# Attention plus gMLP layer on one core: an early pool for the first unit's values, output weights loaded two steps ahead, and four row blocks of the attention output projected among the last units

## The chip, the cores and the metric

The kernel runs on one core of one Trainium2 chip. The metric is the device time of one execution in microseconds (us), the median of three runs. TensorE is written PE, its weight loads PEld, VectorE DVE, ScalarE ACT, GpSimd POOL, and SyncE SP; SPq is SP's instruction queue, from which all the transfers spoken of here are issued.

## The reference, cut to what matters

For 2048 tokens of width 1024, in float32:

```python
y = rms_norm(x, norm_in_g)
q_lat, kv_lat, k_rope, gate_mla, u, v, gate_gmlp = split(y @ w_in)
o_mla  = attention(q_lat, kv_lat, k_rope)          # 8 heads, causal in chunks of 64
o_gmlp = gelu(u) * (w_spatial @ layer_norm(gelu(v)) + b_spatial)
o_mla  = rms_norm(o_mla,  out_norm_mla_g)  * silu(gate_mla)
o_gmlp = rms_norm(o_gmlp, out_norm_gmlp_g) * silu(gate_gmlp)
h = x + concat([o_mla, o_gmlp]) @ w_out
out = rms_norm(h, final_norm_g)
```

## The kernel before, in words

Every product is made of three matmuls on a value split in a high and a low part (`h`, `l`): high by high, high by low, low by high.

**First half** (`with ExitStack() as bs`). Two halves `hf` of 1024 tokens go through the input projections and the low-rank up-projections. Queries, keys and values (high and low) go to DRAM (`qh_d`, `ql_d`, `kh_d`, `kl_d`, `vh_d`, `vl_d`), the gates to `gt_d`. `stage_ug` is the last stage of each half: 8 column chunks by 2 token tiles, each with 48 matmuls (`u` and `g`), 8 small ones (`sp`), and a tail on DVE, ACT and POOL that ends in `zacc`, whose column sums (`zss2`, `zss3`, L87) close the half. The weights of a chunk, `ug0` to `ug7`, lie in `wpool`, three buffers deep. The pool `lp` holds the high and low parts on their way to DRAM. In the second half, ahead of `stage_ug`, the pools on the right side of the memory are closed (`early.close()`) and `kpool`, `qpool` and `mpool` are opened in their room.

**Second half** (`with ExitStack() as at`). Attention goes by 32 units (head `h`, query tile `j` of 512); unit 0 is head 0, tile 3, and the last head goes through its tiles as 3, 2, 1, 0 (units 28 to 31). A unit has `4j + 4` key blocks `kb`: three `ss` matmuls (L793 to L795), exponentials and a split into `ph` and `pl` (ACT, and DVE or POOL by turns), three `po` matmuls (L833 to L835). `ss` has two PSUM buffers. A unit ends in a chain of column sums, reciprocal, `spread` and multiply (`o`, L851), and `o` goes to `ot_d` (L852). `load_unit` loads `ql` (L757), `kl` (L764), `vh` and `vl` (L768) into `vpool`, two units ahead. `row_maxima` makes the row maxima that the exponentials need, some units ahead (`px` on PE, L171; reductions on DVE, L176 and L178).

**What fills PE between key blocks.** After each key block `side()` takes steps of a generator, `filler`: `gmlp_out`, which first makes the gMLP half of the output weights (`out_weights(8)`: load `wos` L865, `woh` on ACT L866, `wol` on DVE L867), then projects the 16 blocks of 128 token rows in 16 steps of three matmuls each (`pg`, L879 to L881) and stores `h1_d`. `tc.issue_after(last.ins)` keeps a step's PE instructions behind that key block's last `ss`. The steps are shared out so that they end with unit 28.

**The end.** After the last unit come `out_weights(0)` and the attention half: `mla_rows(b)` loads `zm` from `ot_d` (L950) and `gm` from `gt_d` (L951), squares, multiplies and splits them (`zmh`, `zml`), and `project` makes block `b` (`pm`, L879 to L881), in the order of the last head's tiles, so the first four blocks are unit 28's rows. Then come the final norm and the store.

**The order of work.** Each queue's order is fixed when the kernel is built: a list scheduler takes, on a simulated timeline, what is ready, earlier lines first; on the chip each queue goes through its list in that order. So a load or a filler step written late can stand early in its queue, and an instruction whose data is late holds up all that stands behind it in its queue.

Of the kernel before, what the change touches and what calls it, by code (L numbers as in the profile page):

```python
# [38 lines left out]
def layer_kernel(ctx: ExitStack, tc: tile.TileContext, a: dict, out: bass.AP):  # L39
# [92 lines left out]
    def load_kh(h, j):  # L132
# [2 lines left out]
        nc.gpsimd.memset(kh[96:100, :].bitcast(F32), 1.0)  # L135
        khs[h, j] = kh

    def max_loads(u):
        h, j = units[u]
        load_qh(h, j)  # L140
        for c in range(j + 1):
            if (h, c) not in khs:
                load_kh(h, c)
# [51 lines left out]
    with ExitStack() as bs:  # L195
# [5 lines left out]
        wpool = pool("wpool", 3)  # L201
        spool = pool("spool", 2)
        tpool = pool("tpool", 2)
        lp = pool("lp", 2)
        up = pool("up", 2)
        early = ExitStack()
        xpool = early.enter_context(tc.tile_pool(name="xpool", bufs=2, side="right"))
        rpool = early.enter_context(tc.tile_pool(name="rpool", bufs=2, side="right"))
        ps_t = early.enter_context(tc.tile_pool(name="ps_t", bufs=3, space=PSUM, side="right"))
        ps_m = pool("ps_m", 5, space=PSUM)  # L210

# [454 lines left out]
        for hf in range(2):  # L666
# [21 lines left out]
            if hf == 1:  # L688
                early.close()
                right_pool("kpool", 7)  # L690
                right_pool("qpool", 6)
                mpool = right_pool("mpool", 3)
                right_pool("ps_x", 2, space=PSUM)
                pools["neg"] = mpool.tile([P, 64], F32, name="neg", bufs=1)
                nc.gpsimd.memset(pools["neg"], NEG)
                pools["mx"] = [mpool.tile([P, 4, 5], F32, name=f"mx{i}", bufs=1) for i in range(3)]
                for m in pools["mx"]:
                    nc.gpsimd.memset(m, NEG)
                pools["mz"] = [mpool.tile([P, P], F32, name=f"mz{i}", bufs=1) for i in range(3)]
                for m in pools["mz"]:  # L700
                    nc.gpsimd.memset(m, 0.0)
            if hf == 0:

                s = spool.tile([P, 1024], F32, tag="stage", name="wsp")
                sv = s.rearrange("p (g t) -> p g t", g=8)
                nc.sync.dma_start(out=sv, in_=a["w_spatial"].rearrange("g s t -> s g t"))
                smask = up.tile([P, P], F32, tag="z", name="smask", bufs=1)
                nc.sync.dma_start(out=smask, in_=a["smask"])
                nc.vector.tensor_mul(sv, sv, smask.unsqueeze(1).broadcast_to([P, 8, P]))
                lnb = spool.tile([P, 1024], F32, tag="stage", name="lnb")  # L710
                nc.sync.dma_start(out=lnb, in_=a["gmlp_ln_b"].partition_broadcast(P))
                diag = rpool.tile([P, 1536], F32, tag="ll", name="diag")
                for c in range(8):
                    nc.vector.tensor_scalar(diag[:, c * P : (c + 1) * P], ident, bsp[:, c : c + 1], None, op0=ALU.mult)
                for g in range(2):
                    pt = ps_t.tile([P, 4, P], F32, tag="pt", name=f"wspt{g}")
                    for i in range(4):
                        nc.tensor.transpose(pt[:, i, :], sv[:, 4 * g + i, :], ident)
                    nc.scalar.copy(wst[:, 4 * g : 4 * g + 4, :], pt)
                for g in range(2):  # L720
                    pt = ps_t.tile([P, 4, P], F32, tag="pt", name=f"rest{g}")
                    for i in range(4):
                        c = 4 * g + i
                        cs = slice(c * P, (c + 1) * P)
                        nc.tensor.matmul(pt[:, i, :], lnb[:, cs], wst[:, c, :], start=True, stop=False)
                        nc.tensor.matmul(pt[:, i, :], ones, diag[:, cs], start=False, stop=True)
                    nc.scalar.copy(rest[:, 4 * g : 4 * g + 4, :], pt)
# [7 lines left out]
    with ExitStack() as at:  # L735
# [2 lines left out]
            return at.enter_context(tc.tile_pool(name=name, bufs=bufs, reuse_waits="tile", **kw))  # L738

        wo = pool("wo", 1)  # L740
        vpool = pool("vpool", 5)
        ppool = pool("ppool", 5)
        wk = pool("wk", 2)
        ep = pool("ep", 1)
# [7 lines left out]

        def load_unit(h, j):

            tok = slice(j * 512, (j + 1) * 512)
            ql = vpool.tile([P, 512], F32R, tag="ql", name=f"ql{h}_{j}", bufs=3)
            nc.sync.dma_start(out=ql[0:QH, :].bitcast(F32), in_=ql_d[h, :, tok])  # L757
            qls[h, j] = ql
            for c in range(j + 1):
                if (h, c) in kls:  # L760
                    continue
                tok = slice(c * 512, (c + 1) * 512)
                kl = vpool.tile([P, 512], F32R, tag="kl", name=f"kl{h}_{c}")
                nc.sync.dma_start(out=kl[0:QH, :].bitcast(F32), in_=kl_d[h, :, tok])  # L764
                kls[h, c] = kl
                vts[h, c] = [vpool.tile([P, 4, P], F32R, tag=tag, name=f"{tag}{h}_{c}") for tag in ("vh", "vl")]
                for dst, src in zip(vts[h, c], (vh_d, vl_d)):
                    nc.sync.dma_start(  # L768
                        out=dst.bitcast(F32),
                        in_=src[tok, h * P : (h + 1) * P].rearrange("(b p) f -> p b f", p=P),  # L770
                    )

        def on_vector(u, nk):

# [82 lines left out]
        nc.vector.tensor_scalar(gout, gout, 0.5, None, op0=ALU.mult)  # L857
        rg = wo.tile([P, NB], F32, name="rg")

        def out_weights(e0):  # L860
            for e in range(e0, e0 + 8):
                s = ep.tile([P, D], F32, tag="ws", name=f"wos{e}", bufs=2)
                wh = wo.tile([P, D], F32R, tag="wh", name=f"woh{e}", bufs=8)
                wl = wo.tile([P, D], F32R, tag="wl", name=f"wol{e}", bufs=8)
                nc.sync.dma_start(out=s, in_=a["w_out"][e * P : (e + 1) * P, :])  # L865
                nc.scalar.activation(wh, s, AF.Copy, scale=gout[:, e : e + 1])  # L866
                nc.vector.scalar_tensor_tensor(  # L867
                    wl, s, gout[:, e : e + 1], wh.bitcast(F32), op0=ALU.mult, op1=ALU.subtract
                )
                yield wh, wl  # L870

        def project(pools, ws, zh, zl, r, xt, nm):
# [19 lines left out]

        def gmlp_out():
            ws = []
            for w in out_weights(8):
                ws.append(w)
                yield
            rsqrt_small(rg, ssz, D, NB)
            for b in range(NB):
# [12 lines left out]
                nc.sync.dma_start(out=h1_d[rows, :], in_=xt)  # L912

        filler = gmlp_out()
        steps = 8 + NB * 16
        weight = [[1 + 6 / (4 * j + 4)] * (4 * j + 4) for _, j in units[: H * NT - 4]]
        weight = [w for ws in weight for w in ws]
        weight += [1.4] * EXTRA
# [7 lines left out]
                next(filler, None)  # L926
                done[1] += 1

        for u in range(2):
            load_unit(*units[u])  # L930
        for u, (h, j) in enumerate(units):
            unit(u, h, j, side)
        for _ in filler:
            pass

        gfin = ep.tile([P, D], F32, tag="zg", name="gfin")
        nc.sync.dma_start(out=gfin, in_=a["final_norm_g"].partition_broadcast(P))
        ws = list(out_weights(0))
        rm = wo.tile([P, NB], F32, name="rm")

        def mla_rows(b):

            rows = slice(b * P, (b + 1) * P)
            zh, zl = [], []
# [1 line left out]
            for g in range(2):  # L946
# [4 lines left out]
                nc.sync.dma_start(out=gm, in_=gt_d[rs, rows].rearrange("(e p) t -> p e t", p=P))  # L951
                nc.scalar.activation(sq[:, 4 * g : 4 * g + 4, :], zm, AF.Square)
                nc.gpsimd.tensor_tensor(zm, zm, gm, op=ALU.mult)
                zh.append(vpool.tile([P, 4, P], F32R, tag="vh", name=f"zmh{b}_{g}"))
                zl.append(vpool.tile([P, 4, P], F32R, tag="vl", name=f"zml{b}_{g}"))
                nc.scalar.copy(zh[g], zm)
                sub_hi(zl[g], zm, zh[g])
            s1 = wk.tile([P, P], F32, tag="s1", name=f"s1_{b}")
# [7 lines left out]
            return zh, zl, xt  # L966

        blocks = [4 * j + k for j in order[H - 1] for k in range(4)]
        ready = mla_rows(blocks[0])
        for n, b in enumerate(blocks):  # L970
            rows = slice(b * P, (b + 1) * P)
            zh, zl, xt = ready
            if n + 1 < NB:
                ready = mla_rows(blocks[n + 1])
            ss = wk.tile([P, 3], F32, tag="fs", name=f"fs{b}")
            junk = ep.tile([P, D], F32, tag="ws", name=f"fj{b}", bufs=2)
            steps = project([px_tile, pe_tile], ws, zh, zl, rm[:, b : b + 1], xt, f"pm{b}")
            for c in range(2):
                cs = slice(512 * c, 512 * c + 512)
                for _ in range(8):  # L980
                    next(steps)
                nc.scalar.activation(junk[:, cs], xt[:, cs], AF.Square, accum_out=ss[:, c : c + 1])
                nc.gpsimd.tensor_scalar(
                    ss[:, 2:3], ss[:, c : c + 1], 1.0 / D, ss[:, 2:3] if c else EPS, op0=ALU.mult, op1=ALU.add
                )
            nc.gpsimd.tensor_tensor(ss[:, 2:3], ss[:, 2:3], mhalf[:, 0:1], op=ALU.pow)
            w = D if n + 1 < NB else 512
            for c in range(0, D, w):
                cs = slice(c, c + w)
                nc.vector.scalar_tensor_tensor(  # L990
                    xt[:, cs], xt[:, cs], ss[:, 2:3], gfin[:, cs], op0=ALU.mult, op1=ALU.mult
                )
                nc.sync.dma_start(out=out[rows, cs], in_=xt[:, cs])


# [68 lines left out]
```

## Time and profile before

| | us |
|---|---|
| median of 3 runs | 1945.61 |
| lowest and highest run | 1943.3 and 1949.13 |
| the profiled execution, its own time | 1944.81 |
| its span, first to last instruction | 1943.0 |
| PE busy in the span | 1888.4 |

The span is 1.8 us shorter than the execution's time. The granted TensorE clock was 0.991 of full speed over the span. A busy PE counts matmuls at either clock, so time lost to a lower clock is busy time too, and is found from the distance between matmuls.

### The profile page before, as it was taken

Reading aid. Unit: us, or ns where it says so; the run is one execution under the profiler, and the core shown is the slowest. Engines: PE = TensorE matmul, PEld = TensorE weight load, DVE = VectorE, ACT = ScalarE, POOL = GpSimd, SP = SyncE. Lnnn points to the kernel's source line nnn. Section 1 sums busy time; section 2 is a strip of 40 time slices with the busy share of each in tenths; the row PEclk is TensorE's granted clock in tenths of the full one; section 3 lists DMA queues with packets and bytes.
Section 4 is the critical chain, followed back from the end, with each engine's and each line's share of the span. In section 5 each row is a group of like instructions: output and inputs, shape, how many; then the busy total and the mean of one; then the engine's idle time right before and its main releaser. Section 6 shows DMA issues by size and latency. Waiting matters only on the chain.

```text
span 1943.0 us, 24726 instructions
## 1 busy us (share of the span) xinstructions
PE 1888.4 (97%) x8558; PEld 1527.0 (79%) x8558; DVE 1166.1 (60%) x2033; ACT 778.0 (40%) x1416; POOL 605.3 (31%) x661
## 2 busy tenths in 40 slices
PE   8999999999999999899998999999999999999998
PEld 6888767888878887688886788888888787767886
DVE  7235454555642454546666877677777777875553
ACT  6232224222422222332213655555555555573332
POOL 5000100122420010001223545554645454564432
PEclk9999999999999999999998999999999999999999
DMA  6226378533322353983216452434425242325652
GB/s 203 93 79 178 95 178 280 148 95 95 103 84 90 86 155 108 233 264 88 85 39 174 130 166 85 125 105 129 124 77 166 71 136 80 95 91 176 196 186 103
DMA packets 238885, 252.44 MB, mean 130 GB/s; under 512 B 18461, under 2 KB 167965, under 8 KB 238761
## 3 DMA queue, kind: packets, MB, share of 16 engines
q1 hardware_dynamic: 238616, 250.86, 43.1%
q8 instruction: 68, 1.11, 0.2%
q14 instruction: 57, 0.46, 0.1%
q10 hardware_dynamic: 144, 0.00, 0.0%
HBM read 158.53 MB, written 92.27 MB: 129 GB/s over the span
## 4 chain that ended last, share of the span: by engine, by line
PE 81%; DVE 6%; DMA 5%; SPq 3%; issue 2%; ACT 2%; POOL 1%; DVEq 0%; POOLq 0%; ACTq 0%
PE px L171 3%; PE po L835 3%; PE ss L793 3%; PE ss L794 3%; PE pm L880 3%; PE pm L881 3%; PE ss L795 3%; PE pm L879 3%; PE po L833 3%; PE pg L879 3%; PE po L834 3%; PE g L112 3%; PE u L111 3%; PE u L110 3%; PE u L112 3%; PE g L110 3%
## 5 line engine op out<-in xcount | busy, mean ns | idle before, releaser
L178 DVE TENSOR_REDUCE mx<-px 128x1 f32<-128x512 f32 (+2 forms) x320 | 178.5, 579 | 19.8 <-PE px L171 17.4
L831 POOL TENSOR_TENSOR accg<-accg,p 128x512 f32<-128x512 f32 (+1 forms) x104 | 119.1, 1145 | 191.2 <-ACT p L825 141.5
L827 POOL TENSOR_TENSOR pl<-p,ph 128x512 fp32r<-128x512 f32 (+1 forms) x128 | 153.4, 1199 | 40.6 <-ACT ph L826 30.2
L77 DVE TENSOR_TENSOR pl<-ss,ph 128x512 fp32r<-128x512 f32 (+2 forms) x160 | 92.8, 580 | 109.7 <-ACT ss L809 103.9
L604 POOL TENSOR_TENSOR z<-gu,ggt 128x512 f32<-128x512 f32 x32 | 41.5, 1295 | 367.4 <-DVE gu L602 200.3
L808 ACT ACTIVATE ph<-ss 128x512 fp32r<-128x512 f32 (+2 forms) x160 | 81.9, 512 | 128.9 <-PE ss L795 119.6
L835 PE MATMUL po<-pl,vh 128*128 128x512 f32 (+1 forms) x320 | 122.6, 383 | 2.4 <-POOL pl L827 1.5
L793 PE MATMUL ss<-qh,kh 100*128 100x512 f32 (+1 forms) x320 | 121.5, 380 | 3.3 <-ACT p L825 3.1
L833 PE MATMUL po<-ph,vh 128*128 128x512 f32 (+1 forms) x320 | 120.5, 376 | 3.7 <-ACT ph L808 3.5
L794 PE MATMUL ss<-ql,kh 96*128 96x512 f32 (+1 forms) x320 | 119.2, 372 | 0.0
L795 PE MATMUL ss<-qh,kl 96*128 96x512 f32 (+1 forms) x320 | 118.0, 369 | 0.0
L834 PE MATMUL po<-ph,vl 128*128 128x512 f32 (+1 forms) x320 | 117.5, 367 | 0.0
L171 PE MATMUL px<-kh,qh 96*128 96x512 f32 (+2 forms) x320 | 110.1, 386 | 6.8 <-DVE mx L178 5.2
L110 PE MATMUL gm<-yh,wh_gm 128*128 128x512 f32 x256 | 101.0, 395 | 4.8 <-DVE kf L402 3.8
L880 PE MATMUL pm<-wol,zmh 128*128 128x512 f32 x256 | 102.2, 399 | 0.0
L881 PE MATMUL pm<-woh,zml 128*128 128x512 f32 x256 | 101.0, 396 | 0.9 <-DVE zml L77 0.9
L879 PE MATMUL pg<-woh,zgh 128*128 128x512 f32 x256 | 101.6, 397 | 0.0
L879 PE MATMUL pm<-woh,zmh 128*128 128x512 f32 x256 | 101.5, 396 | 0.0
L110 PE MATMUL u<-yh,wh_ug 128*128 128x512 f32 x256 | 101.4, 396 | 0.0
L881 PE MATMUL pg<-woh,zgl 128*128 128x512 f32 x256 | 100.8, 394 | 0.0
L880 PE MATMUL pg<-wol,zgh 128*128 128x512 f32 x256 | 100.8, 394 | 0.0
L112 PE MATMUL gm<-yh,wl_gm 128*128 128x512 f32 x256 | 100.5, 392 | 0.0
(713 smaller groups left out, 5021.5 us busy)
## 6 DMA issues: line engine op xcount, KB each, us to landing
ws_ug<-in_w_in SPq DMA_DIRECT2D x32, 512.0 KB, 5.2
xt<-in_x_t SPq DMA_DIRECT2D x16, 512.0 KB, 4.7
gv_d<-gv SPq DMA_DIRECT2D x32, 256.0 KB, 2.0
ws_gm<-in_w_in SPq DMA_DIRECT2D x16, 512.0 KB, 4.2
gt_d<-gth SPq DMA_DIRECT2D x32, 256.0 KB, 2.8
lgv<-gv_d SPq DMA_DIRECT2D x32, 256.0 KB, 2.9
z_d<-z SPq DMA_DIRECT2D x32, 256.0 KB, 2.6
vh<-vh_d SPq DMA_DIRECT2D x32, 256.0 KB, 4.0
```

The lines of the kernel that those rows point to most:

```text
L110: nc.tensor.matmul(ps, wh(d), xh(d), start=(d == 0), stop=False)
L112: nc.tensor.matmul(ps, wl(d), xh(d), start=False, stop=(d == n - 1))
L178: nc.vector.reduce_max(mx[:, b, c + 1 : c + 2], px[:, :w], axis=AX.X)
L793: nc.tensor.matmul(ss[:, l0:], kh[0:100, ks], qh[0:100, l0:], start=True, stop=False)
L794: nc.tensor.matmul(ss[:, l0:], kh[0:QH, ks], ql[0:QH, l0:], start=False, stop=False)
L795: last = nc.tensor.matmul(ss[:, l0:], kl[0:QH, ks], qh[0:QH, l0:], start=False, stop=True)
L833: nc.tensor.matmul(po[:, v0:], vh[:, vs, :], ph[:, v0:], start=(kb == 0), stop=False)
L834: nc.tensor.matmul(po[:, v0:], vl[:, vs, :], ph[:, v0:], start=False, stop=False)
L835: nc.tensor.matmul(po[:, v0:], vh[:, vs, :], pl[:, v0:], start=False, stop=(kb == nk - 1))
L879: nc.tensor.matmul(ps, h, ws[d][0][:, cs], start=(d == 0), stop=False)
L880: nc.tensor.matmul(ps, h, ws[d][1][:, cs], start=False, stop=False)
L881: nc.tensor.matmul(ps, lo, ws[d][0][:, cs], start=False, stop=(d == 7))
```

## The change

It does three things, and moves pools for them.

1. A pool `vfirst` (one buffer of each tag) is opened on the right side after `early.close()`, and ahead of the last `stage_ug` it gets unit 0's `ql` and chunk 0 of head 0's `kl`, `vh` and `vl`. `vpool` goes from 5 buffers to 4 (3 to 2 for `ql`), and each fifth chunk (third `ql`) goes to `vfirst`. `lp` moves to the right side, among the pools that `early.close()` frees, so all pools of the second half lie 8 KB lower in each partition, over other tiles of the first half than before.
2. `out_weights` issues the load of tile `e + 2` after the conversion of tile `e`, instead of each load ahead of its own conversion. For the gMLP half six empty filler steps stand between the first two loads and the first conversion (14 steps instead of 8).
3. `mla_out` is the loop of the end as a generator. Its beginning (`gfin`, `out_weights(0)`, `mla_rows` of the first block) stands ahead of unit 29, and units 29, 30 and 31 take 3, 2 and 3 of its steps after each key block: 12 x 3 + 8 x 2 + 4 x 3 = 64 steps, four blocks of 16. The split rows of the blocks up to number 4, and of every second block behind, lie in `ep` (`zh`, `zl`, room for one block), the others in `vpool`.

The diff, cut to its core:

```diff
+    FIRST = 1
+    def load_ql(h, j):
+        if (h, j) in qls:
+            return
+        pool, bufs = (pools["vfirst"], 1) if len(qls) % 3 == 0 else (pools["vpool"], 2)
+        ql = pool.tile([P, 512], F32R, tag="ql", name=f"ql{h}_{j}", bufs=bufs)
+        nc.sync.dma_start(out=ql[0:QH, :].bitcast(F32), in_=ql_d[h, :, j * 512 : (j + 1) * 512])
+        qls[h, j] = ql
+
+    def load_chunk(h, c):
+        if (h, c) in kls:
+            return
+        pool = pools["vfirst" if len(kls) % 5 < FIRST else "vpool"]
...
-        lp = pool("lp", 2)
...
+        lp = early.enter_context(tc.tile_pool(name="lp", bufs=2, side="right"))
...
                 early.close()
                 right_pool("kpool", 7)
                 right_pool("qpool", 6)
+                right_pool("vfirst", 1)
                 mpool = right_pool("mpool", 3)
...
+                load_ql(*units[0])
+                for c in range(FIRST):
+                    load_chunk(units[0][0], c)
...
-        vpool = pool("vpool", 5)
+        vpool = pools["vpool"] = pool("vpool", 5 - FIRST)
...
         def load_unit(h, j):
...
+            load_ql(h, j)
             for c in range(j + 1):
+                load_chunk(h, c)
...
-        def out_weights(e0):
+        def out_weights(e0, wait=0):
+            loaded = []
+            def load(e):
+                s = ep.tile([P, D], F32, tag="ws", name=f"wos{e}", bufs=2)
+                nc.sync.dma_start(out=s, in_=a["w_out"][e * P : (e + 1) * P, :])
+                loaded.append(s)
+            load(e0)
+            load(e0 + 1)
+            for _ in range(wait):
+                yield None
             for e in range(e0, e0 + 8):
-                s = ep.tile([P, D], F32, tag="ws", name=f"wos{e}", bufs=2)
+                s = loaded[e - e0]
...
-                nc.sync.dma_start(out=s, in_=a["w_out"][e * P : (e + 1) * P, :])
...
+                if e + 2 < e0 + 8:
+                    load(e + 2)
                 yield wh, wl
...
-            for w in out_weights(8):
-                ws.append(w)
+            for w in out_weights(8, 6):
+                if w:
+                    ws.append(w)
                 yield
...
-        steps = 8 + NB * 16
+        steps = 14 + NB * 16
...
-        def mla_rows(b):
+        def mla_rows(n, b):
...
-                zh.append(vpool.tile([P, 4, P], F32R, tag="vh", name=f"zmh{b}_{g}"))
-                zl.append(vpool.tile([P, 4, P], F32R, tag="vl", name=f"zml{b}_{g}"))
+                turn = n > 4 and n % 2
+                for zs, tag in ((zh, "h"), (zl, "l")):
+                    pool, kw = (vpool, {}) if turn else (ep, {"bufs": 2})
+                    zs.append(pool.tile([P, 4, P], F32R, tag=("v" if turn else "z") + tag, name=f"zm{tag}{b}_{g}", **kw))
...
+        def mla_out():
+            gfin = ep.tile([P, D], F32, tag="zg", name="gfin")
+            nc.sync.dma_start(out=gfin, in_=a["final_norm_g"].partition_broadcast(P))
+            ws = list(out_weights(0))
+            ready = mla_rows(0, blocks[0])
+            yield
+            for n, b in enumerate(blocks):
+                zh, zl, xt = ready
+                if n + 1 < NB:
+                    ready = mla_rows(n + 1, blocks[n + 1])
...
+                    for _ in range(8):
+                        next(steps)
+                        yield
...
+        rows_of = {H * NT - 3: 3, H * NT - 2: 2, H * NT - 1: 3}
+        for u, (h, j) in enumerate(units):
+            if u not in rows_of:
+                unit(u, h, j, side)
+                continue
+            if u == min(rows_of):
+                for _ in filler:
+                    pass
+                next(mla)
+            unit(u, h, j, lambda: [next(mla) for _ in range(rows_of[u])])
+        for _ in mla:
+            pass
```

## Rows read from the trace of the kernel before

**Rows 1.** Part 1 of the page: busy time of PE over the span.
```profile
PE 1888.4 (97%) x8558; PEld 1527.0 (79%) x8558; DVE 1166.1 (60%) x2033; ACT 778.0 (40%) x1416; POOL 605.3 (31%) x661
```

**Rows 2.** Windows: us; busy us (count) PE, PEld, DVE, ACT, POOL; clock, DMA share, GB/s.
```profile
1043.40:1053.70 10.30, 6.34 (x27) 4.41 (x26) 9.07 (x21) 2.55 (x3) 2.53 (x2) 0.69 0.92 245
...
1061.90:1071.40 9.50, 5.98 (x17) 4.13 (x16) 7.33 (x11) 6.41 (x10) 2.56 (x2) 0.64 1.05 353
1071.40:1100.00 28.60, 25.70 (x115) 19.22 (x114) 23.89 (x38) 21.36 (x37) 18.62 (x16) 1.00 0.58 177
1100.00:1500.00 400.00, 400.00 (x1906) 326.46 (x1905) 294.31 (x622) 228.67 (x488) 208.23 (x225) 1.00 0.37 115
...
1700.00:1733.00 33.00, 30.51 (x141) 23.05 (x140) 27.47 (x53) 26.72 (x53) 21.98 (x22) 1.00 0.33 110
1733.00:1752.50 19.50, 15.96 (x80) 11.96 (x79) 12.95 (x29) 13.83 (x34) 12.57 (x16) 1.00 0.27 82
1752.50:1780.00 27.50, 26.48 (x117) 20.93 (x116) 13.36 (x20) 5.49 (x11) 10.38 (x13) 1.00 0.39 117
```

**Rows 3.** Timeline of PE, start of attention: start, us, instruction, [idle before <- releaser].
```profile
1053.74 0.63 PE L793 MATMUL ss<-qh,kh 100*128 100x512 f32 x1
...
1057.57 0.39 PE L795 MATMUL ss<-qh,kl 96*128 96x512 f32 x1
...
1060.38 0.40 PE L793 MATMUL ss<-qh,kh 100*128 100x512 f32 x1
1060.62 0.40 PE L794 MATMUL ss<-ql,kh 96*128 96x512 f32 x1
...
1065.82 0.80 PE L833 MATMUL po<-ph,vh 128*128 128x512 f32 x1 [3.52 <-ACT ph L808]
...
1071.35 0.40 PE L835 MATMUL po<-pl,vh 128*128 128x512 f32 x1
...
1079.95 0.40 PE L879 MATMUL pg<-woh,zgh 128*128 128x512 f32 x1
```

**Rows 4.** Waits of all engines, 1040 to 1100: total us, times, longest.
```profile
PE px L171 <- DVE mx L178: 3.9, 4, 1.9
```

**Rows 5.** Timeline of SP's queue, start of attention.
```profile
1043.26 0.32 SPq L764 DMA_DIRECT2D kl<-kl_d  x1
...
1055.27 1.30 SPq L865 DMA_DIRECT2D wos<-in_w_out  x2
```

**Rows 6.** Waits of SP's queue, 1030 to 1100.
```profile
SPq L764 <- PE g L111: 5.1, 1, 5.1
```

**Rows 7.** Chain that ended last, 1043 to 1110: start, us, what.
```profile
1055.27 7.52 DMA wos<-in_w_out
...
1080.70 3.71 DMA wos<-in_w_out
```

**Rows 8.** Timeline of ACT, start of attention.
```profile
1050.05 1.28 ACT L825 ACT_TABLE_LOAD   x1
```

**Rows 9.** Timeline of SP's queue, ahead of the last stage_ug.
```profile
849.84 1.18 SPq L334 DMA_DIRECT2D ws_ug<-in_w_in  x1
```

**Rows 10.** Chain that ended last, 815 to 872: end of the first ug chunk.
```profile
870.62 0.89 PE sp L595 x8
```

**Rows 11.** Timeline of SP's queue, last units.
```profile
1726.22 13.52 SPq L852 DMA_DIRECT2D ot_d<-o  x2
1739.79 8.15 SPq L950 DMA_DIRECT2D zm<-ot_d  x3
```

**Rows 12.** Timeline of PE, the first matmul of the attention half's projection.
```profile
1749.72 0.50 PE L879 MATMUL pm<-woh,zmh 128*128 128x512 f32 x1
```

**Rows 13.** Tile zm: ns min/median/max of one, and time from issue to landing.
```profile
L953 POOL TENSOR_TENSOR zm<-zm,gm x32: 1272/1299/1771, 1747.7 to 1911.0; 128x512 f32<-128x512 f32 x32
...
DMA to landing us min/median/max: 2.7/3.3/6.1
```

**Rows 14.** Part 6 of the page: transfers by line, KB each, median us to landing.
```profile
ot_d<-o SPq DMA_DIRECT2D x32, 256.0 KB, 2.5
```

More of the change, by code (lines that the diff above doesn't have):

```diff
@@ L136, in load_kh @@
         khs[h, j] = kh
+    FIRST = 1
[10 more added lines that the diff above has]
+        pool = pools["vfirst" if len(kls) % 5 < FIRST else "vpool"]
+        tok = slice(c * 512, (c + 1) * 512)
+        kl = pool.tile([P, 512], F32R, tag="kl", name=f"kl{h}_{c}")
+        nc.sync.dma_start(out=kl[0:QH, :].bitcast(F32), in_=kl_d[h, :, tok])
+        kls[h, c] = kl
+        vts[h, c] = [pool.tile([P, 4, P], F32R, tag=tag, name=f"{tag}{h}_{c}") for tag in ("vh", "vl")]
+        for dst, src in zip(vts[h, c], (vh_d, vl_d)):
+            nc.sync.dma_start(
+                out=dst.bitcast(F32),
+                in_=src[tok, h * P : (h + 1) * P].rearrange("(b p) f -> p b f", p=P),
+            )
     def max_loads(u):
@@ L753, in load_unit @@
         def load_unit(h, j):
[L755 to L758, printed above, removed]
+            load_ql(h, j)
             for c in range(j + 1):
[L760 to L771, printed above, removed]
+                load_chunk(h, c)
         def on_vector(u, nk):
@@ L927, in side @@
                 done[1] += 1
[L929 to L938, printed above, removed]
         rm = wo.tile([P, NB], F32, name="rm")
-        def mla_rows(b):
+        def mla_rows(n, b):
             rows = slice(b * P, (b + 1) * P)
@@ L968, in layer_kernel @@
         blocks = [4 * j + k for j in order[H - 1] for k in range(4)]
[L969 to L993, printed above, removed]
@@ new lines, in mla_out @@
+        def mla_out():
[5 more added lines that the diff above has]
+            for n, b in enumerate(blocks):
+                rows = slice(b * P, (b + 1) * P)
+                zh, zl, xt = ready
+                if n + 1 < NB:
+                    ready = mla_rows(n + 1, blocks[n + 1])
+                ss = wk.tile([P, 3], F32, tag="fs", name=f"fs{b}")
+                junk = ep.tile([P, D], F32, tag="ws", name=f"fj{b}", bufs=2)
+                steps = project([px_tile, pe_tile], ws, zh, zl, rm[:, b : b + 1], xt, f"pm{b}")
+                for c in range(2):
+                    cs = slice(512 * c, 512 * c + 512)
+                    for _ in range(8):
+                        next(steps)
+                        yield
+                    nc.scalar.activation(junk[:, cs], xt[:, cs], AF.Square, accum_out=ss[:, c : c + 1])
+                    nc.gpsimd.tensor_scalar(
+                        ss[:, 2:3], ss[:, c : c + 1], 1.0 / D, ss[:, 2:3] if c else EPS, op0=ALU.mult, op1=ALU.add
+                    )
+                nc.gpsimd.tensor_tensor(ss[:, 2:3], ss[:, 2:3], mhalf[:, 0:1], op=ALU.pow)
+                w = D if n + 1 < NB else 512
+                for c in range(0, D, w):
+                    cs = slice(c, c + w)
+                    nc.vector.scalar_tensor_tensor(
+                        xt[:, cs], xt[:, cs], ss[:, 2:3], gfin[:, cs], op0=ALU.mult, op1=ALU.mult
+                    )
+                    nc.sync.dma_start(out=out[rows, cs], in_=xt[:, cs])
@@ new lines, in layer_kernel @@
+        for u in range(2):
+            load_unit(*units[u])
+        mla = mla_out()
+        rows_of = {H * NT - 3: 3, H * NT - 2: 2, H * NT - 1: 3}
[10 more added lines that the diff above has]
+            pass
```

## The prediction

> **What bounds the kernel now.** I read the page first: PE is busy for 1888.4 us of a span of 1943.0 [rows 1], so 54.6 us are idle, and no other engine comes near it. The change leaves every matmul in place; it can only give back time in which PE stood idle or ran at the lower clock, in the stretches that it touches. So the second view is the busy time by stretch [rows 2]. From 1100 to 1500 PE is busy for 400.00 of 400 us: nothing is to be had there, and a denser filler changes nothing. Two places are left.
>
> The first is the start of attention. In 1043.4 to 1053.7 PE idles 10.30 - 6.34 = 3.96 us, in 1061.9 to 1071.4 it idles 9.50 - 5.98 = 3.52, and in 1071.4 to 1100 it idles 28.60 - 25.70 = 2.90 [rows 2]. The granted clock in the first two is 0.69 and 0.64, a mix of the two levels of 1.2 and 2.4 GHz, behind stretches in which PE waited. What that costs is read from the distance of matmuls [rows 3]. At full clock a 512-column matmul follows the last in 0.24 us (1060.38 to 1060.62). From 1053.74 to 1057.57 eight such matmuls and two small ones took 3.83 us, and 8 x 0.24 + 0.2 = 2.1 would do: 1.7 lost. From 1065.82 to 1071.35 twelve and a small one took 5.53, and 3.0 would do: 2.5 lost. So the start loses 3.96 + 1.7 = 5.7, then 3.5 + 2.5 = 6.0, then 2.9: 14.6 us.
>
> The second place is the last units: 33.00 - 30.51 = 2.49 us idle in 1700 to 1733, 19.50 - 15.96 = 3.54 in 1733 to 1752.5 and 27.50 - 26.48 = 1.02 in 1752.5 to 1780, at full clock [rows 2]. Here attention runs with no filler left. The idle share of the first of these, 2.49 / 33 = 7.5%, is my price for attention without filler.
>
> Then the waits say why. In the first hole PE had only row maxima to do and waited 3.9 us for DVE's reductions [rows 4], because the first key chunk is issued at 1043.26 [rows 5], after SP had stood 5.1 us for the last reader of the weights in whose room it lies [rows 6]. The first `ss` stands at 1053.74. The second hole, 3.52 us at 1065.82, is a wait for ACT [rows 3], and ACT stood at the first weight conversion: its load, issued at 1055.27, took 7.52 us, against 3.71 for one issued at 1080.70 [rows 7].
>
> **The change, part by part.**
>
> *Early pool.* Unit 0's `ql` and chunk 0 are 96 x 512 x 4 bytes twice and 128 x 512 x 4 twice, 0.92 MB, at 245 GB/s [rows 2] 3.7 us of transfer taken out of the full queue. They are issued some 190 us earlier, ahead of `stage_ug`. There SP may stand at them until `lp`'s last stores have left, and the weights of the next ug chunk come later by that and by 3.7 us. The cover: those are issued at 849.84 [rows 9], and the first chunk's matmuls end at 870.62 [rows 10]; with some 5 us for the load, 15 us are spare. I price this at 0; beyond 15 us it would show one for one. With the data there, `ss` of key blocks 0 to 3 can follow the last `sp` at about 1044. Chunk 1 still lies in room of the last ug weights and is issued at about 1043.3, which is early enough for key block 4. What remains in the first stretch of 14.2 us: 7.5% of it for attention without filler (1.1), the table load of 1.28 that now stands ahead of the first exponential with PE waiting [rows 8], and 0.6 for a short spell at the lower clock: 3.0. The ends are 0 and the 5.7 of now. Gain 2.7.
>
> *Weights two steps ahead.* The conversions need the same ACT and DVE time. What goes is the 7.52 us landing, if the two loads get clear of the unit loads: 3.7 us less stand ahead of them, and the hole was 3.52. The scheduler may still put a conversion into a gap of ACT where its simulated load has landed, so I leave 0.8 for a rest of it, and 7.5% of 9.5 us, 0.7: 1.5 of 6.0 remain. The ends are 0 and 6.0. Gain 4.5. The first `pg` matmul comes at 1079.95, 26.2 us after the first `ss` [rows 3]; with 14 steps instead of 8 it comes some seven key blocks later in program order, while attention starts nine us earlier, so about 1075 to 1080 again. In 1071.4 to 1100 I keep 7.5%, 2.1 of 2.9. Gain 0.8. Start together: 8.0.
>
> One rule of the Trainium skill speaks against this part. The rows: 7.52 us at 1055.27, with the DMA engines at 0.92 to 1.05 of their time around it, against 3.71 later [rows 2, 7]. The Trainium skill, "DMA: Bandwidth & Descriptors", section "Queues, rings and completion order", says that a DMA engine takes the descriptors of one ring in their order. By that rule alone the weights come no sooner than all that SP issued ahead of them, and the sum would lack the 4.5.
>
> *Four blocks among the last units.* The matmuls are the same; 64 steps move from behind the last unit to between the key blocks of units 29 to 31. They can start when unit 28's output has gone through DRAM: it is stored at 1726.22, but the read behind it in SP's queue stands until 1739.79, after unit 29's store [rows 11]. With the read written ahead of unit 29 it follows at 1726.2 + 2.5 for the store [rows 14], and 3.3 for the read and 1.3 on POOL [rows 13], then two short passes on ACT and DVE: about 1734.5, against 1749.72 for the first `pm` now [rows 12]. So 1700 to 1733 stays as it is (0), and of the 3.54 behind it I keep 1.0. Gain 2.5; the ends are a gain of 3.54 and the loss of the rival below. Of the 1.02 behind, 0.7. `ep` holds split rows for one block, but the first half is read for the last time 12 matmuls (2.8 us) ahead of a block's end, and key blocks stand by: 0. The extra ACT, DVE and POOL work beside the last units is work that moved; DVE is busy for 12.95 of 19.50 us there [rows 2], so it has room. The tail after the last matmul stays.
>
> **Sum.** 1944.8 (the profiled execution, 0.8 below the median shown) - 8.0 - 2.5 - 0.7 = 1933.6, so 1934 us. What a measurement can tell from no change is 0.3%, 5.8 us.
>
> **Rivals.**
>
> *The weights stay late.* `ep` now lies 8 KB lower, over tiles that the end of `stage_ug` still uses, so the loads of `wos` may be issued no earlier, and the queue is still full; ACT stands again. Then the second stretch keeps its 6.0, the first gives 2.0, the third 0.5, the end 3.2: 1944.8 - 5.7 = 1939.1. For it: the 7.52 us. Against it: 3.7 us less in the queue. This is where the page's rule leads. Chance 0.20.
>
> *Slower: PE stands at the projection.* The order is fixed ahead, so `pm` matmuls stand in PE's queue where the simulated rows are ready. If the real ones are late, PE and all attention behind stand. At worst the first block waits for store and read, 2.5 + 3.3, the three others for a read each, 3 x 3.3, and all four for POOL, 4 x 1.3: 20.9 us, and the 3.2 at the end is gone: 1944.8 - 8.0 + 20.9 = 1957.7. It ends slower by over 0.3% from 8.0 + 5.8 = 13.8 us of such waits. For it: an in-order queue that ACT's stand of now shows to be costly. Against it: unit 28's chain sits in the same queues, so its lateness moves the rest too. Chance 0.10.
>
> *Much more.* Nearly all holes close: 21.6 us lost in all, of which some 4 stay: 1927. Against it: the 7.5% without filler. Chance 0.08.
>
> *The order does not follow.* Data are early, but the first `ss` stays behind the row maxima and column sums in PE's list, and the weights stay late: 1944.8 - 2 = 1943. Chance 0.04.
>
> **How the numbers follow.** The forecast has the remaining 0.58; its own range is 1929 to 1939. Faster: 0.52 of the forecast, half of the first rival and the third, 0.70. Same: the rest of these two and the fourth, 0.06 + 0.10 + 0.04 = 0.20. Slower: 0.10. For eight in ten the range goes from 1927 (the third rival) to 1946 (the lightest end of the slower case): below it some 0.05, above it some 0.09.
>
> **What would show it.** Right: a first `ss` near 1044.5 on the time scale of before, no idle of PE over 1 us behind `ph` at ACT's first conversion, a clock of 0.9 or more from 1043 to 1071, `pm` matmuls from about 1735 of that scale between `ss` and `po`, and no change of the time up to `stage_ug`'s end. Wrong: SP late with `ws_ug` and PE idle between 850 and 1043; ACT idle for `wos` again; PE idle at `pm` for `zmh` or `zml`; or a first `ss` behind `zss3`.

## The result, and the profile after

The changed kernel takes 1963.34 us (median of 4 runs, 1961.63 to 1966.05) against 1944.91 for the kernel before, run beside it: ratio 1.0083, 95% interval [1.0067, 1.0100]. It is 0.8% slower; 1934 was predicted, in a range of 1927 to 1946. The profiled execution has a span of 1959.8 us, 16.8 above that of before.

Busy time by stretch of the changed kernel, with the columns of [rows 2]:

```profile
core 0: us, PE busy (x) PEld busy (x) DVE busy (x) ACT busy (x) POOL busy (x), PEclk, DMA share, GB/s
1043.40:1053.70 10.30, 6.27 (x27) 4.34 (x26) 8.75 (x21) 2.54 (x3) 2.52 (x2) 0.74 0.91 231
1061.90:1071.40 9.50, 6.70 (x17) 4.49 (x17) 8.46 (x13) 7.90 (x13) 4.79 (x3) 0.69 0.90 304
1071.40:1100.00 28.60, 25.82 (x102) 19.64 (x101) 21.82 (x36) 21.06 (x38) 19.41 (x16) 0.87 0.53 159
1100.00:1500.00 400.00, 400.00 (x1908) 327.00 (x1907) 292.73 (x620) 227.24 (x485) 207.50 (x222) 1.00 0.38 115
...
1710.00:1740.00 30.00, 18.11 (x65) 12.74 (x65) 19.75 (x38) 13.05 (x24) 10.30 (x10) 0.85 0.45 138
...
1840.00:1860.00 20.00, 13.44 (x50) 10.21 (x49) 13.78 (x17) 7.04 (x16) 11.03 (x16) 0.74 0.49 151
```

The kernel before, in the two stretches at the end that [rows 2] does not have:

```profile
1710.00:1740.00 30.00, 27.91 (x127) 20.77 (x126) 22.67 (x48) 23.21 (x48) 20.95 (x19) 1.00 0.17 60
...
1840.00:1860.00 20.00, 20.00 (x90) 16.21 (x89) 11.30 (x13) 7.44 (x16) 7.85 (x12) 1.00 0.58 184
```

Against [rows 2] the first hole is as it was: 6.27 busy of 10.30, where it was 6.34. The second has 6.70 instead of 5.98. In 1071.4 to 1100, 102 matmuls run instead of 115, at a granted clock of 0.87 instead of 1.00. Two new holes stand at the end: 30.00 - 18.11 = 11.9 us idle in 1710 to 1740 (30.00 - 27.91 = 2.1 before, over the same times), and 20.00 - 13.44 = 6.6 in 1840 to 1860 (none before). From 1100 to 1500 PE is busy all the time, as before.

These holes are not the whole account. It is read from the distance between two places that both kernels have: the last `sp`, and the column sums of unit 28 (`pzs28t`, 1712.33 before and 1716.28 after). From the last `sp` to these sums 669.1 us became 672.7. From the sums to the last matmul, before, after, and with only the place of one tile changed (b1 below):

```profile
1712.33:1935.79 223.46, 217.68 (x962) 172.96 (x960) 123.33 (x174) 85.91 (x187) 96.03 (x137) 1.00 0.47 150
```

```profile
1716.28:1952.43 236.15, 218.99 (x966) 178.05 (x966) 127.16 (x174) 87.49 (x190) 97.69 (x137) 0.96 0.45 143
```

```profile
1716.75:1936.09 219.34, 213.39 (x962) 172.88 (x960) 123.46 (x174) 85.77 (x187) 96.40 (x137) 1.00 0.47 153
```

The end takes 12.7 us longer than before: idle time goes from 5.8 to 17.2 us (the two holes add 16.4, and 5 of the idle time before is gone elsewhere), and busy time rises by 1.3. Against b1, which has the tiles where the changed kernel has them, busy time rises by 5.6 us for the same matmuls: that is the lower clock, 0.85 and 0.74 in the stretches of the holes.

**The first hole.** PE's timeline of the changed kernel:

```profile
1043.59 1.05 PE L622 MATMUL sp<-wst,lgv 128*128 128x128 f32 x8
...
1047.37 0.50 PE L198 MATMUL px<-kh,qh 96*128 96x512 f32 x1 [1.88 <-DVE mx L205]
...
1052.56 1.06 PE L87 MATMUL zss3t<-ident,zacc 128*128 128x128 f32 x4
...
1054.06 0.63 PE L811 MATMUL ss<-qh,kh 100*128 100x512 f32 x1
```

The early loads are all issued by 865.43 and land long before, yet the first `ss` stands at 1054.06 (1053.74 in [rows 3]): it follows the last `sp`, nine row maxima and the column sums `zss3` in PE's list, as it did before. That nothing in its data holds it is shown by b3.

**The first new hole.** ACT's timeline of the changed kernel:

```profile
1718.64 1.15 ACT L896 ACTIVATE woh<-wos,gout 128x1024 fp32r<-128x1024 f32 x1 [2.90 <-DMA wos<-in_w_out]
1719.69 0.61 ACT L975 ACTIVATE sq<-zm 128x512 f32<-128x512 f32 x1
1722.25 0.62 ACT L982 CAST zmh<-zm 128x512 fp32r<-128x512 f32 x1 [1.95 <-POOL zm L976]
1722.78 0.59 ACT L843 ACTIVATE p<-ss 128x512 f32<-128x512 f32 x1
...
1735.95 0.63 ACT L975 ACTIVATE sq<-zm 128x512 f32<-128x512 f32 x1 [10.95 <-DMA zm<-ot_d]
1736.49 0.58 ACT L843 ACTIVATE accg<-ss 128x512 f32<-128x512 f32 x1
```

and SP's queue there:

```profile
1730.81 0.32 SPq L870 DMA_DIRECT2D ot_d<-o  x1
1733.18 1.47 SPq L973 DMA_DIRECT2D zm<-ot_d  x3
```

Unit 29's first exponential (`p`, 1722.78) is behind the last weight conversion (2.90 us of waiting) and behind `sq` and `zmh` of block 12 (1.95). Its third (`accg`) is behind a second `sq`, whose rows are in unit 28's output: stored at 1730.81, read at 1733.18. ACT stands 10.95 us for it, and everything of unit 29 with it. PE's own long waits here are 3.9 us at `pzm`, for a row maximum that stands in DVE's list behind the last weight's low part and `zml`, and 4.1 at `ss`, for that `accg` (both in the list of waits below).

The store itself is hardly later in its own chain. Unit 28's normalization stands on PE behind twelve `pm` matmuls that begin at 1724.01, and DVE waits 3.77 us for it, but from `pzs28t` to the store it is 14.5 us, where it was 13.9 before (1712.33 to 1726.22 in [rows 11]); the other 4.0 were lost ahead of `pzs28t`. What is new is that ACT's list has the late rows ahead of unit 29's exponentials.

**The second new hole.** DVE's timeline, then waits of PE from 1700 to 1860 (total, times, longest), of which the first line belongs to this hole and the other two to the first:

```profile
1838.00 0.68 DVE L97 TENSOR_TENSOR rr<-pzr31r,pick 8x512 fp32r<-8x512 f32 x1 [4.66 <-PE pzr31r L96]
1841.86 0.69 DVE L869 TENSOR_TENSOR o<-pzr31b,o 128x512 f32<-128x512 f32 x1 [3.18 <-PE pzr31b L104]
...
1844.13 2.73 DVE L916 SCALAR_TENSOR_TENSOR h<-pm,rm,h 128x512 f32<-128x512 f32 x4 [0.31 <-POOL rm L81]
1846.78 1.94 DVE L985 TENSOR_REDUCE s<-sq 128x128 f32<-128x1024 f32 x1
```

```profile
PE pr L987 <- DVE s L985: 5.5, 2, 5.1
PE pzm L175 <- DVE mz L209: 4.6, 2, 3.9
PE ss L811 <- ACT accg L843: 4.1, 1, 4.1
```

DVE twice stands for PE (4.66, 3.18) in the middle of unit 31's chain, whose PE steps are spread among `pm` matmuls. Four evacuations of `pm` (x4 at 1844.13) and the sum for the next block's `pr` are behind it in DVE's list. ACT stands too, 23.95 us until 1844.97, ahead of the squares of these `h` and of the next block's `sq`. So PE runs out of work: 5.1 us at `pr`.

### The profile page after: what moved, and what is told of

Its sections match the earlier page's. It is cut to its first block, busy times and chain, and to the rows that moved or that the text cites. A ratio compares the mean times of both kernels' runs of the same rounds, so it can differ in the third digit from the quotient of the medians.

```text
span 1959.8 us, 24713 instructions
## 1 busy us (share of the span) xinstructions
PE 1894.4 (97%) x8558; PEld 1536.2 (78%) x8558; DVE 1165.0 (59%) x2033; ACT 778.2 (40%) x1416; POOL 610.3 (31%) x661
## 4 chain that ended last, share of the span: by engine, by line
PE 81%; DVE 5%; DMA 4%; SPq 4%; issue 2%; ACT 2%; POOL 2%; DVEq 0%; POOLq 0%; ACTq 0%
PE po L853 3%; PE ss L811 3%; PE po L851 3%; PE ss L812 3%; PE px L198 3%; PE ss L813 3%; PE po L852 3%; PE pm L912 3%; PE pg L911 3%; PE pg L912 3%; PE pm L913 3%; PE pg L913 3%; PE pm L911 3%; PE g L112 3%; PE u L110 3%; PE u L111 3%
## 5 line engine op out<-in xcount | busy, mean ns | idle before, releaser
L845 POOL TENSOR_TENSOR pl<-p,ph 128x512 fp32r<-128x512 f32 (+1 forms) x128 | 158.1, 1235 | 43.0 <-ACT ph L844 31.7
```

## The experiments

Times of the same place differ between executions by some us from the first half alone (the last `sp` begins at 1040.26 to 1048.40), so idle times of a stretch and distances are compared, and gains by the ratios. Every ratio is to the kernel before on the same chip; 0.001 is 1.95 us. The distance from the last `sp` to `pzs28t` and that from `pzs28t` to the end of the span are read from one execution each; the kernel before, taken twice, has 669.1 and 671.2, and 230.7 and 230.9.

**One part at a time** (a1 to a4): the changed kernel with the other parts taken back; all four keep the small tile `rm` ahead of the output weights, as the changed kernel has it (see b1). Without the early pool (a2, a3), without the weights' part (a1, a3) and without the blocks among the last units (a1, a2, a4) its lines become:

```
-        pool = pools["vfirst" if len(kls) % 5 < FIRST else "vpool"]
+        pool = pools["vpool"]
...
-        steps = 14 + NB * 16
+        steps = 8 + NB * 16
...
-        rows_of = {H * NT - 3: 3, H * NT - 2: 2, H * NT - 1: 3}
+        rows_of = {}
```

> The early pool alone, weights and order of the end as before. Theory O (PE's order): the first ss stands behind zss3's column sums in PE's list whenever its data come, so nothing is gained: 1.000 of before within 0.003, first ss at 1054 +/- 1, as before. Rival T (transfers): the early loads clear the queue and the weights land sooner, which the changed kernel lost again by its two-steps-ahead loads: 3 to 6 us faster, with ACT's stand at the first woh under 1 us.

Measured: 0.9980 [0.9968, 0.9991]; first `ss` at 1054.88, 10.5 us after the last `sp` as before. Theory O holds for the order. Rival T has the time right, but ACT's stand at the first `woh` is 3.32 us, not under 1; the 3.9 us are explained by b1.

> The weights fetched two steps ahead alone. Theory O: the conversion still waits in ACT's list where the plan put it, and the first loads leave at 1055 as before; same within 0.003, or 1 to 3 us slower, since the eight weight steps come with six empty steps and pg begins later. Rival T: the second hole of 6.0 us closes by 3 us or more, so 3 to 5 us faster.

Measured: 1.0002 [0.9992, 1.0013]. Against b1, which has `rm` early as this run has, it is 3.5 us slower.

> The projection among the last units alone, start as before. Theory E (the end carries the whole loss): the changed kernel's unit 28 ended its sums 4.0 us later than before and its end was 18.4 us later, so the end costs 14.4: 12 to 17 us slower, ratio 1.006 to 1.009. Rival (the parts interact, the early pool or the denser buffers make the rows late): under 8 us slower.

Measured: 1.0041 [1.0027, 1.0055], 8 us, below the expected 12 to 17 and at the edge of the rival. By b1 3.1 us of gain are hidden in it, so the end alone costs 11 by the ratios (14.5 in the profiled execution, the slowest of its eight: 241.0 from `pzs28t` to the end against b1's 226.5). In the changed kernel the same part costs 16 (1.0083 against 1.0001 of a4). Its first hole is 8.5 us, not 11.9: here `accg` stands ahead of the second `sq` in ACT's list and comes at 1729.68. PE's wait for it is 1.62 us instead of 4.10; the wait for the row maximum stays, 3.54 instead of 3.91.

> Early pool and weights two ahead, the end as before. Theory E: 1 to 4 us slower than before (unit 28's sums came 4.0 us later in the changed kernel), ratio 1.000 to 1.002. Rival (the start's loss is only the profiled run's, the start gains by the median): 2 to 8 us faster.

Measured: 1.0001 [0.9991, 1.0011]: no gain from the start. So the end carries the loss.

**What the early pool's gain was** (b1).

```
+        rm = wo.tile([P, NB], F32, name="rm")
...
-        rm = wo.tile([P, NB], F32, name="rm")
```

> The kernel before with one thing of the changed one: the small tile rm (64 bytes a partition) is made ahead of the output weights' tiles, not behind them, so these lie 64 bytes higher. Theory P (placement): the pm matmuls of the last stretch, alone on PE, average 395, 401 and 395 ns in the kernel before and 390, 396 and 389 ns in all five profiles that have rm early; 768 x some 5.7 ns = 4.4 us, so ratio 0.9978 +/- 0.0010, and the early pool's 0.998 was this and not the pool. Rival (the one profile of before, or another chip): 1.000 +/- 0.001, and the pool's gain of 3.9 us is its own.

Measured: 0.9984 [0.9972, 0.9996], 3.1 us. The early pool alone is 0.0004 better than this: nothing that can be told from zero. The traces agree on the place: from `pzs28t` to the end it is 230.7 and 230.9 us in the two profiles of the kernel before and 226.2 to 227.3 in the eight runs that have `rm` early and no projection among the last units (a1, a2, a4, b1 to b3, c4, d4). The prediction gave the place of this tile no thought.

**The order of PE's list** (b2 without, b3 with the early pool; both with `rm` early).

```
         for t in (2, 3):
-            column_sums(mm_tile, zaccs[t], ...)
+            column_sums(px_tile, zaccs[t], ...)
```

> As b1, and the column sums zss2 and zss3 take their PSUM tile from the row maxima's pool instead of the first half's, with no early pool. Theory O (the first half's PSUM pool is only free for attention when its last tile, zss3's, is read, and zss3 waits for POOL): the first ss now stands ahead of zss3 and of nine of the eleven row maxima and moves from 1053 to about 1049 to 1051, where it waits for its late loads: 1 to 4 us faster than b1. Rival (data, not order, hold the first ss): as b1 within 0.001.

> As b2 with the early pool, so data and order are both there. Theory O: first ss near 1046 to 1047, attention's first unit fills the first hole: 4 to 8 us faster than b1, at least 2 faster than b2; this is what the prediction meant the early pool to give. Rival: the same as the early pool alone within 0.002, because the wait for DVE's row maxima or ACT's weights only moves.

Measured: 0.9978 [0.9969, 0.9988] and 0.9959 [0.9945, 0.9974]. PE's timeline of b2, then of b3, then the stretch of b3:

```profile
1048.40 1.05 PE L625 MATMUL sp<-wst,lgv 128*128 128x128 f32 x8
...
1050.29 0.73 PE L809 MATMUL ss<-qh,kh 100*128 100x512 f32 x2 [0.41 <-DVE mix L627]
...
1055.56 1.11 PE L87 MATMUL zss3t<-ident,zacc 128*128 128x128 f32 x4 [3.17 <-POOL zacc L641]
```

```profile
1042.99 1.05 PE L625 MATMUL sp<-wst,lgv 128*128 128x128 f32 x8
...
1044.88 0.50 PE L814 MATMUL ss<-qh,kh 100*128 100x512 f32 x1 [0.41 <-DVE mix L627]
...
1050.66 0.66 PE L87 MATMUL zss3t<-ident,zacc 128*128 128x128 f32 x4
```

```profile
1043.40:1053.70 10.30, 8.42 (x40) 5.69 (x39) 6.10 (x12) 6.94 (x11) 5.25 (x5) 1.00 0.92 242
```

In both the first `ss` follows the last `sp` by 1.9 us instead of 10.5. Without the early loads b2 then stands for `zss3` (3.17) and has only two key blocks to do; with them b3 goes on at a granted clock of 1.00. Against b1 the gains are 1.2 and 4.9 us (by the distance from the last `sp` to `pzs28t`, 670.2 in b1, 668.5 and 665.6). Order and data are each worth little alone. The edit changes nothing but the pool of the sums' PSUM tile, so that is what held attention's first `ss` back.

**The end, begun later** (b4).

```
-        rows_of = {H * NT - 3: 3, H * NT - 2: 2, H * NT - 1: 3}
+        rows_of = {H * NT - 2: 4, H * NT - 1: 8}
```

> The changed kernel with the projection begun ahead of unit 30 instead of 29 (4 steps a key block in unit 30, 8 in unit 31). Theory A (late rows stand ahead of unit 29's exponentials on ACT and ot_d reads behind a late store): PE's 12 us idle in 1710 to 1740 goes to under 4, so 7 to 11 us faster than the changed kernel, 5 to 9 slower than before. Rival B (any projection among the last units costs as much, since the rows are late wherever they are put): the hole only moves to unit 30 or 31, and the time stays within 3 us of the changed kernel, 1.007 or more of before.

Measured: 0.9986 [0.9976, 0.9996], some 19 us below the changed kernel by the ratios: more than theory A expected, since the second hole goes too. From `pzs28t` to the end it takes 224.3 us, where a4, without blocks among the last units, takes 226.2; by the ratios it is 2.9 us below a4, and the intervals overlap. Its windows:

```profile
1710.00:1740.00 30.00, 26.38 (x119) 19.74 (x119) 24.76 (x49) 23.94 (x50) 22.30 (x22) 0.99 0.38 113
...
1830.00:1860.00 30.00, 29.80 (x134) 24.36 (x134) 20.42 (x25) 12.09 (x25) 16.98 (x24) 1.00 0.70 220
```

**SP's stands taken away** (c3).

```
-            nc.sync.dma_start(out=ot_d[...], in_=o)
+            (nc.gpsimd if u >= H * NT - 4 else nc.sync).dma_start(out=ot_d[...], in_=o)
```

> The changed kernel with the ot_d stores of units 28 to 31 issued by POOL, so that SP stands at none of them. Theory S (SP's stand at the late stores holds the reads behind them): the two holes at the end shrink by the stands, 16 us at unit 31's store and 7 at unit 28's, and 5 to 10 us of the 18 come back. Theory L (the rows are late because ACT's, DVE's and PE's lists hold them and the chains of units 28 and 31): the holes stay, within 3 us of the changed kernel, 1.007 or more of before.

Measured: 1.0077 [1.0065, 1.0089], as the changed kernel. Both holes stay:

```profile
1710.00:1740.00 30.00, 17.83 (x54) 12.02 (x54) 17.80 (x34) 10.23 (x17) 10.94 (x10) 0.72 0.40 121
...
1830.00:1860.00 30.00, 22.80 (x94) 17.86 (x93) 15.71 (x23) 7.04 (x16) 11.73 (x18) 0.83 0.34 104
```

Theory S falls: SP's stands at the stores hold nothing that PE needs sooner.

**One hole or two** (d1): the rows begun at key block 6 of unit 29.

```
-                next(mla)
+                plan = iter([0] * 6 + [1] + [7] * 5)
+                unit(u, h, j, lambda: [next(mla) for _ in range(next(plan))])
+                continue
```

> The changed kernel with weights and first rows begun at key block 6 of unit 29, then 7 steps a key block, units 30 and 31 as in the changed kernel. Two-cause theory (unit 29's exponentials behind late rows on ACT make the first hole; unit 31's chain among pm steps on PE and DVE makes the second): the first hole shrinks by 6 to 10 us, the second stays near 6: 1.003 to 1.006 of before. One-cause theory (the second hole follows from the first's lateness): both vanish, 0.998 to 1.001 as with the later begin.

Measured: 1.0042 [1.0027, 1.0058]. The first hole is nearly gone (2.7 us idle), the second stays (6.9):

```profile
1710.00:1740.00 30.00, 27.26 (x118) 19.92 (x117) 23.64 (x47) 19.03 (x36) 15.46 (x15) 1.00 0.47 145
...
1830.00:1860.00 30.00, 23.10 (x96) 18.22 (x95) 16.88 (x20) 9.43 (x21) 14.13 (x21) 0.89 0.48 149
```

Two causes, then: the late rows ahead of unit 29's exponentials, and unit 31's chain among the `pm` steps. That DVE's place of that chain makes the second hole is read from the timeline; no run moved the chain alone.

**The first step in the changed kernel itself** (d2): the changed kernel with the edit of b2.

> The changed kernel with nothing but the zss sums' PSUM tile moved to the row maxima's pool. Order theory: first ss near 1046 instead of 1054, and 4 to 6 us faster than the changed kernel, 1.004 to 1.006 of before. Rival (the six empty steps and the later pg take the gain away): within 2 us of the changed kernel, 1.007 or more.

Measured: 1.0038 [1.0024, 1.0053], 8.8 us below the changed kernel by the ratios (intervals apart). It is more than b3 gained; the difference is within the intervals. The first `ss` is at 1045.61, 1.9 us behind the last `sp`, and the distance to `pzs28t` falls from 672.7 to 667.5, 5.2 us.

**The empty steps** (c4 against a2): two ahead without the six empty steps.

```
-            for w in out_weights(8, 6):
+            for w in out_weights(8):
...
-        steps = 14 + NB * 16
+        steps = 8 + NB * 16
```

> The kernel before with rm early and the weights two ahead, without the six empty steps. Theory W: 0.998, as rm early alone (0.9984), and 3 us faster than with the empty steps (1.0002). Rival (fetching two ahead costs by itself): 1.000 within 0.001.

Measured: 0.9962 [0.9947, 0.9977], 7.8 us below a2 and 4.3 below b1, where the intervals still touch. The first `pg` matmul of a2, then of c4:

```profile
1093.41 0.40 PE L906 MATMUL pg<-woh,zgh 128*128 128x512 f32 x1
```

```profile
1081.30 0.40 PE L906 MATMUL pg<-woh,zgh 128*128 128x512 f32 x1
```

So the six empty steps cost: they leave attention 12 us longer without filler, and from the last `sp` to `pzs28t` a2 takes 674.0 us and c4 669.8. That fetching two ahead gains by itself is not shown: c4's ratio is below b1's by more than theory W expected, but b1 has 670.2 over the same distance, and ACT stands 3.33 us for the first weights in c4 and 3.19 in b1.

**The best parts together** (c1: the early pool with the edits of b1, b2 and b4, weights one ahead; c2: the same with two ahead as in c4, without empty steps).

> Early pool, zss sums in the row maxima's PSUM pool, projection begun ahead of unit 30, weights one ahead as before. If the gains add: pool and sums gave 0.9959, and the later begin stood 0.0015 below the start of the changed kernel alone (0.9986 against 1.0001), so 0.994 to 0.995, some 10 us faster than before. Rival (an earlier start only brings unit 28's chain to the same late rows, gains do not add): 0.996 or more.

> As c1 with the weights fetched two steps ahead but without the six empty steps. Theory W (two ahead is harmless, the six empty steps cost 3 us by delaying pg): as c1 within 0.001, 1 to 2 us faster if ACT's wait for the weights shrinks. Rival (fetching two ahead costs by itself, as both runs with it stood 3 us above those without): 2 to 4 us slower than c1.

Measured: 0.9944 [0.9932, 0.9956] and 0.9945 [0.9933, 0.9957]. c1 takes 1936.29 us against 1947.90: it beats both kernels. The gains add, as c1's first theory had it. Two ahead adds nothing here either.

**The place of the weights' tiles** (d3 the kernel before again, d4 `rm` early and a tile more).

```
+        pad = wo.tile([P, NB], F32, name="pad")
```

> The kernel before, unchanged, one more look. Placement theory: pm matmuls in the last stretch again 395, 401 and 395 ns. Rival (chance of that execution): 390, 396 and 389.

> The kernel before with rm and one more 64-byte tile ahead of the output weights, so they lie 128 bytes higher than before. If the place modulo 128 bytes decides: 395, 401, 395 ns as before. If any higher place helps, or place has no part: 390, 396, 389.

Groups of PE's instructions from 1880 to 1920 (count, busy us, mean ns), d3 and then d4:

```profile
L880 PE MATMUL pm<-wol,zmh 128*128 128x512 f32 x57 | 22.8, 401 | 0.0
L881 PE MATMUL pm<-woh,zml 128*128 128x512 f32 x57 | 22.5, 395 | 0.0
L879 PE MATMUL pm<-woh,zmh 128*128 128x512 f32 x56 | 22.1, 395 | 0.0
```

```profile
L895 PE MATMUL pm<-wol,zmh 128*128 128x512 f32 x58 | 22.9, 395 | 0.0
L894 PE MATMUL pm<-woh,zmh 128*128 128x512 f32 x58 | 22.6, 390 | 0.0
L896 PE MATMUL pm<-woh,zml 128*128 128x512 f32 x58 | 22.6, 389 | 0.0
```

The kernel before has 401, 395, 395 a second time, so it is no chance of one execution, and 128 bytes higher is as good as 64: the place modulo 128 is not it.

## Why the prediction was wrong

In the profiled executions the 16.8 us are made up so: 3.6 between the last `sp` and `pzs28t`, which is the size of the six empty steps (3.5 for a2 against b1, by the ratios); 12.7 from there to the last matmul, which are 11.4 more idle time and 5.6 at the lower clock, less 4.3 for the place of `rm`; 0.3 ahead of `sp` and 0.2 in the tail. By the ratios the end costs 16 (changed against a4) and the start with its empty steps and with `rm` 0.2 (a4): together 16.1. Added up from the runs of one part alone (11 for the end in a3, 3.5, less 3.1 and 0.8) it would be 10.7 only: each of these is uncertain by some 3 us, and the end costs less in a3, where `accg` stands elsewhere in ACT's list. The prediction's gain of 8.0 at the start was nothing, and its gain of 3.2 at the end was a loss.

- *"With the data there, `ss` of key blocks 0 to 3 can follow the last `sp`"*: this step failed. Data were one of two conditions; the other was the order of PE's list, set by a PSUM tile that the diff does not touch. The text had this as the rival "The order does not follow", at 0.04, and put its sign ("a first `ss` behind `zss3`") among the things that would show it wrong. With it fell the reading that the late first key chunk left PE with row maxima alone: in a1 the chunk is early and the 10.5 us stay. The gain of this part, once order and data are both there, was rated too low: 4.9 us in b3 against 2.7; for the whole start nothing reached the 8.0.
- *Early pool at no cost for SP*: right. From 845 to 1043 PE is busy for 198.00 of 198.00 us in both kernels.
- *"The first `pg` matmul ... about 1075 to 1080 again"*: failed with the first step on which it rested; it came at 1094.86. The term "0.8 gained in 1071.4 to 1100" became a loss: 13 matmuls fewer in that stretch.
- *The second hole*, 4.5 of 6.0 gained: failed at *"if the two loads get clear of the unit loads"*. 0.7 us of idle time went (9.50 - 6.70 = 2.80, where it was 3.52), and the clock was still 0.69. ACT's wait for the first weights went from 3.57 to 2.26 us and PE's from 3.52 to pieces of 1.03, 1.09 and 0.68. The two loads leave at 1054.84 (1055.27 in [rows 5]), and the conversion starts 6.6 us later, where 7.52 was the landing [rows 7]. Where 0.92 MB had been taken out of the queue, two loads of gates (`gm`, 256 KB each), which the kernel before issues behind these weights, now stand directly ahead of them:

```profile
1052.99 1.54 SPq L974 DMA_DIRECT2D gm<-gt_d  x2
1054.84 1.97 SPq L885 DMA_DIRECT2D wos<-in_w_out  x2
```


The Trainium skill, "DMA: Bandwidth & Descriptors", section "Queues, rings and completion order", says that a DMA engine takes the descriptors of one ring in their order. The trace does not speak against that; no run put these loads on another ring.
- *"1700 to 1733 stays as it is (0)"*: this step failed, and it decided. The text asked when the rows could be there (about 1734.5) and took it that nothing would stand before; they were there at about that time (the second `sq` begins at 1735.95), but in the lists `sq`, `zmh` and `pm` of block 12 stand ahead of unit 29's work, and PE was at `pm` by 1724.01. Idle time in 1710 to 1740 went from 2.1 to 11.9 us; with the rows begun six key blocks later it is 2.7 (d1). The text costed late rows as PE standing at `pm`; what stood was ACT, with unit 29's exponentials behind it.
- *The extra work "beside the last units is work that moved"*, with no price behind 1780: the second step that failed. 6.6 us of idle time came in 1840 to 1860, where DVE has the next rows behind unit 31's chain, and after both holes matmuls ran at the lower clock (5.6 us in all). *"key blocks stand by: 0"*, said of the room for split rows, held nearly: ACT's one wait of that kind is 1.5 us, for `zmh` at 1741.60.
- *The slower rival* had the right end and a price of the right size (20.9 at worst; 17.0 measured, 11.4 idle and 5.6 at the lower clock), but a chance of 0.10 and not this mechanism, so the price is in part luck; its 1957.7 still kept the 8.0 of the start. The reason given against it, that unit 28's chain sits in the same queues and its lateness moves the rest too, did not hold: from `pzs28t` to its store that chain took 14.5 us instead of 13.9, and ACT stood all the same, because its list had the rows first.
- *SP's queue*, whose standing from 1726.22 to 1739.79 [rows 11] the text took for what holds the read, is not what decides in the changed kernel: c3.

## What to carry to other kernels

Here data that came early gained nothing until the first instruction that uses them also stood early in its engine's list; look at what shares its PSUM banks or buffers, here one column sum's tile. Work that depends on a round trip through DRAM, put between steps of a pipeline whose engines go through fixed lists, was paid here on the engine whose list has it ahead of the pipeline's next step (ACT, and by the timeline DVE), not on the one that uses it; begun twelve key blocks later (b4), it cost nothing. When a part gains, check that the gain is not from its neighbours in the diff: 3.1 of the early pool's 3.9 us came from a 64-byte tile. And look at the pace as well as at the holes: a third of what the end lost was time in which PE was busy.

## What was not expected of the hardware

With the output weights' tiles 64 or 128 bytes higher, the `pm` matmuls, alone on PE, average 390, 395 and 389 ns instead of 395, 401 and 395; over 768 of them that is 4.4 us; the stretch from `pzs28t` to the end is 4.2 us shorter in b1, and b1's ratio gives 3.1. The `pg` matmuls, which read tiles at the same places between attention's matmuls, show no difference (393 to 397 ns in either). Why is open.
